# Nine of the 22 gate/value pairs of a feed-forward up-projection by seven block products in place of eight

## The chip, the cores and the metric

The kernel runs on one core of one Trainium2 chip. The metric is device time in microseconds (us) of one execution. Three runs of the kernel before took 861.26, 861.86 and 863.12 us; the median is 861.86 us.

## The reference

One block of a network on x of 512 rows (SEQ) and 1024 columns (D). A mixer (an mLSTM, an S5 state-space branch and their output product) takes up the first half of the time and is not touched. After it comes a feed-forward part with 2816 hidden channels, which are 22 groups of 128; the convolution has three taps along the rows:

```python
h = _standardize(x) * (1.0 + sc2) + sh2
val, gate = jnp.split(h @ w_ffn_up, 2, axis=-1)
gate = jax.nn.gelu(_causal_dwconv(gate, w_ffn_conv, b_ffn_conv))
f = (gate * val) @ w_ffn_down
x = _layer_norm(ALPHA * x + (1.0 + g2) * f, ln2_gain, ln2_bias)
```

All data are 32-bit floats.

## The kernel before, in words

**Products in three parts.** TensorE multiplies operands in the type fp32r. To keep the precision of 32 bits, each operand is split into a high part and a rest: ScalarE casts it (L221, `split_into`), VectorE subtracts the cast from the original (L210, `sub`). `mm3` (L241 to L244) then makes high x high, high x rest and rest x high, all added into one PSUM bank. A weight tile is loaded from DRAM into a `w` tile (SyncE starts the load, L192) and split into `wh` and `wl` (`wsplit`), 128 partitions x 1024 each.

**The up-projection.** `h2` holds the eight transposed activation tiles (128 channels x 512 rows each, as high part and rest; in the pools `s5b`, `s5h` and `hx`). A *unit* is one group of 128 output channels: `up_mm` makes 8 contraction blocks x 3 matmuls of 512 columns. Two units make a *pair* j: first the gate unit 2j+1 into a bank `acc`, then the value unit 2j into a bank `hd`. The first four units (pairs 0 and 1, `early`) are made in two halves of 256 columns, since the second half of the rows is transposed later.

`gate_half` (L1180 on) takes the gate from PSUM: ScalarE copies it to SBUF (L1184) and makes the last tap with its bias (L1186), VectorE adds two taps (L202), then `gelu2` (L561 to L565) goes ScalarE Square (L562), VectorE, ScalarE Tanh (L564), VectorE. `val_half` multiplies by the value bank (L207) and splits the product into a high part and a rest, which stay in SBUF until the down-projection reads them.

```python
for j in range(NF):
    ...
    for u in (2 * j + 1, 2 * j):
        ...
            w = wsplit(h["wup"][u])
            ou[u] = bank("acc" if u % 2 else "hd")
            up_mm(ou[u], w, slice(0, 512))
        if u % 2:
            gg = gate_half(j, ou[u])
    val_half(j, gg, ou[2 * j])
    if 8 <= j < 16:
        ada2_step(1)
```

`ada2_step` makes an eighth of a modulation vector on VectorE (two L202 passes into `s5h`); `grow` (at `G2J`) turns that vector into a row for all partitions, which scales the down-projection's weights.

**The down-projection.** `tail_product` goes through the 22 blocks in order and multiplies the scaled weights with the stored products, into all eight PSUM banks; the last eight blocks' weights are held resident, and the result goes through the norm row tile by row tile.

**What sets the order.** The program order of each engine is settled when the kernel is built, by the framework's scheduler from the order of the code, and each engine then works strictly in that order, with semaphore waits between engines. Pools limit how far engines run ahead: `w` 2 buffers, `wh` and `wl` 3 each, `gab` 4, `hh` 7, and of the eight PSUM banks `acc` 2, `s5` 2, `hd` 4.

## Time and profile before

| | |
|---|---|
| median of 3 runs | 861.86 us (861.26 to 863.12) |
| the profiled execution: its span | 862.0 us |
| TensorE (PE) busy | 828.5 us, 96% |
| VectorE (DVE) busy | 607.1 us, 70% |
| ScalarE (ACT) busy | 368.6 us, 43% |
| GpSimd (POOL) busy | 98.0 us, 11% |
| DMA queue, share of 16 engines | 36.0% |
| chain that ended last | PE 76%, DVE 11%, ACT 4%, DMA 4% |

The span goes from the first to the last instruction of one execution under the profiler; what lies around it is within the spread of the three runs, so the span is compared with the median as it stands. Busy shares are means over stages with different limits. The chain is the work that ended last, followed back from the last instruction to what released each step. In a timeline a row gives start, length, engine, line, operation, output <- inputs, and in brackets the idle time of the engine before it and what ended that.

### The profile page before, as it was taken

The numbers are of one execution on the slowest core, as the hardware profiler recorded it, in microseconds if no ns is written. First come the engines' busy times: TensorE is split into PE (matmuls) and PEld (weight loads), VectorE is DVE, ScalarE is ACT, GpSimd is POOL, SyncE is SP. The second block draws the span as 40 slices with busy tenths as digits, with TensorE's granted clock in tenths as the row PEclk, the third lists the DMA queues.
The fourth block names the chain that finished last, engine by engine and source line by source line (L and its number), as shares of the span: only waits on it lengthen the run. The fifth ranks groups of instructions, "written<-read, shape, count | busy, mean of one in ns | idle before, by whom it ended". The sixth has DMA issues, their size and how long they took to land.

```text
span 862.0 us, 11353 instructions
## 1 busy us (share of the span) xinstructions
PE 828.5 (96%) x4106; PEld 669.2 (78%) x4106; DVE 607.1 (70%) x1144; ACT 368.6 (43%) x589; POOL 98.0 (11%) x255
## 2 busy tenths in 40 slices
PE   3999999999999999999999999999999999999996
PEld 1777868778777778888887988888888878888785
DVE  5557978788689774578978767556777675878144
ACT  4454573564556442232334555444444444333000
POOL 2781211122022100000002200000000000000000
PEclk9999999999999999999999999999999999999998
DMA  9832132122222233568655023224444232445011
GB/s 336 288 132 86 53 101 62 45 85 62 79 60 87 86 123 122 196 203 294 210 191 177 2 74 102 94 98 147 146 147 137 86 120 74 171 163 169 11 49 49
DMA packets 45415, 105.94 MB, mean 123 GB/s; under 512 B 13360, under 2 KB 14256, under 8 KB 45360
## 3 DMA queue, kind: packets, MB, share of 16 engines
q1 hardware_dynamic: 45360, 105.23, 36.0%
q8 instruction: 32, 0.52, 0.2%
q14 instruction: 23, 0.19, 0.1%
HBM read 101.01 MB, written 2.10 MB: 120 GB/s over the span
## 4 chain that ended last, share of the span: by engine, by line
PE 76%; DVE 11%; ACT 4%; DMA 4%; issue 2%; SPq 2%; POOL 0%; DVEq 0%; ACTq 0%; POOLq 0%
PE acc L242 11%; PE acc L243 11%; PE acc L244 11%; PE hd L242 11%; PE hd L243 11%; PE hd L244 11%; DVE hh L202 2%; SPq L192 2%; DVE s5h L207 1%; PE s L242 1%; PE s L244 1%; PE s L243 1%; DVE wl L210 1%; PE s L612 1%; DMA w<-in_wmix 1%
## 5 line engine op out<-in xcount | busy, mean ns | idle before, releaser
L221 ACT CAST wh<-w 128x1024 fp32r<-128x1024 f32 (+2 forms) x103 | 103.2, 1003 | 144.0 <-PE acc L243 111.5
L210 DVE TENSOR_TENSOR wl<-w,wh 128x1024 fp32r<-128x1024 f32 (+2 forms) x103 | 120.5, 1172 | 60.8 <-ACT wh L221 60.1
L242 PE MATMUL acc<-hp,wh 128*128 128x512 f32 x256 | 103.4, 405 | 0.5 <-ACT hx L785 0.5
L244 PE MATMUL acc<-hp,wl 128*128 128x512 f32 x256 | 102.1, 399 | 0.0
L243 PE MATMUL acc<-hp,wh 128*128 128x512 f32 x256 | 102.1, 399 | 0.0
L242 PE MATMUL hd<-s5b,wh 128*128 128x512 f32 (+1 forms) x168 | 63.4, 380 | 0.7 <-ACT s5b L1169 0.5
L243 PE MATMUL hd<-s5b,wh 128*128 128x512 f32 (+1 forms) x168 | 63.6, 379 | 0.2 <-DVE s5b L210 0.2
L244 PE MATMUL hd<-s5b,wl 128*128 128x512 f32 (+1 forms) x168 | 63.3, 378 | 0.0
L242 PEld LDWEIGHTS acc<-hp,wh 128*128 128x128 f32 x256 | 48.2, 189 | 14.7 <-issue 3.7
L202 DVE SCALAR_TENSOR_TENSOR hh<-hh,hh 128x512 f32<-128x512 f32 x52 | 35.9, 691 | 31.2 <-ACT hh L564 14.7
L244 PEld LDWEIGHTS acc<-hp,wl 128*128 128x128 f32 x256 | 48.4, 189 | 11.2 <-issue 0.4
L243 PEld LDWEIGHTS acc<-hp,wh 128*128 128x128 f32 x256 | 48.4, 189 | 10.8 <-issue 0.4
L202 DVE SCALAR_TENSOR_TENSOR s5h<-hh,k,s5h 128x512 f32<-128x512 f32 x56 | 39.3, 746 | 4.7 <-DMA hh<-in_wa 4.6
L242 PEld LDWEIGHTS hd<-s5b,wh 128*128 128x128 f32 x168 | 31.3, 188 | 7.6 <-ACT s5b L1169 0.8
L243 PEld LDWEIGHTS hd<-s5b,wh 128*128 128x128 f32 x168 | 31.7, 189 | 7.0 <-DVE s5b L210 0.6
L244 PEld LDWEIGHTS hd<-s5b,wl 128*128 128x128 f32 x168 | 31.6, 188 | 6.4
L202 DVE SCALAR_TENSOR_TENSOR hh<-hh,k,hh 128x512 f32<-128x512 f32 x44 | 33.0, 751 | 4.5 <-ACT hh L1186 3.6
L1024 POOL TENSOR_SCALAR mov<-mov 128x1 f32<-128x1 f32 x6 | 3.7, 624 | 276.2 <-ACT s L1023 159.6
L244 PE MATMUL acc<-hx,wl 128*128 128x512 f32 x84 | 33.1, 394 | 0.0
L242 PE MATMUL acc<-hx,wh 128*128 128x512 f32 x84 | 33.1, 394 | 0.0
L243 PE MATMUL acc<-hx,wh 128*128 128x512 f32 x84 | 33.1, 394 | 0.0
L244 PE MATMUL acc<-s5b,wl 128*128 128x512 f32 x80 | 31.6, 395 | 0.5 <-DVE wl L210 0.5
(547 smaller groups left out, 2053.1 us busy)
## 6 DMA issues: line engine op xcount, KB each, us to landing
w<-in_wup SPq DMA_DIRECT2D x44, 512.0 KB, 3.2
hh<-in_wa SPq DMA_DIRECT2D x64, 256.0 KB, 4.2
w<-in_win SPq DMA_DIRECT2D x30, 512.0 KB, 3.2
w<-in_wfd SPq DMA_DIRECT2D x22, 512.0 KB, 3.3
hb<-in_wa SPq DMA_DIRECT2D x16, 512.0 KB, 7.4
w<-in_wglu SPq DMA_DIRECT2D x8, 512.0 KB, 3.3
w<-in_wdn SPq DMA_DIRECT2D x8, 512.0 KB, 3.3
w<-in_wmix SPq DMA_DIRECT2D x8, 512.0 KB, 4.2
```

The costliest lines, as they stand in the source:

```text
L192: return nc.sync.dma_start(o, i)
L202: V.scalar_tensor_tensor(o, i0, s, i1, op0=op0, op1=op1)
L207: V.tensor_tensor(o, a, b, op=op)
L210: V.tensor_tensor(o, a, b, op=ALU.subtract)
L221: A.copy(hi, x)
L242: T.matmul(o, lhsT=wh, rhs=xh, start=first, stop=False)
L243: T.matmul(o, lhsT=wh, rhs=xl, start=False, stop=False)
L244: T.matmul(o, lhsT=wl, rhs=xh, start=False, stop=last)
L612: T.matmul(o, lhsT=F[:, ri, pr, :], rhs=XB[:, ri, pr].rearrange("p g k -> p (g k)"), start=ri == 0, stop=False)
L1024: GP.tensor_scalar(v[:, 2:3], v[:, 0:1], v[:, 1:2], EPS * D, op0=ALU.add, op1=ALU.add)
```

## The change

The two units of a pair have the same eight activation tiles as their other operand. With the contraction cut into two halves and the 512 rows cut into two halves, a pair is a product of two 2 x 2 block matrices: the weights A11, A12 (gate, first and second half of the contraction), A21, A22 (value) and the activations B. For nine pairs (`FAST`) `fast_pair` makes it by seven block products, in Winograd's form of Strassen's scheme, in place of eight; a product (`prod`) is 4 contraction blocks x 3 matmuls of 256 columns.

- Four combinations of the weights per pair (S1 to S4), each 128x512, on GpSimd (`gtt`); the weights are loaded into the pool `gab`. Seven weight blocks are then split (`half`), each 128x512, in the pools `wh` and `wl` in turn.
- Four combinations of the activations, made and split once when pair 2 begins (`x_combos`), from raw activations that are now kept (`xraw`); they fill four buffers of `hp` (their splits are `xd`).
- Order of the products: a = A11 B11; copy of a into bank b by ScalarE; c = S3 X3; copy of c to SBUF; b += S2 X2; then VectorE adds b and c into bank d; a += A12 B21; b += S1 X1; VectorE adds b and c again (v); d += A22 X4; b += S4 B22. The gate is a (first half of the rows) and b (second half), the value d and v. Bank b is an `acc` bank, d an `s5` bank, by the parity of j; a and c are `hd` banks.
- `gate_half` reads the gate from PSUM where it stands in one bank, and copies it from two banks where it doesn't; its first tap is shortened at the edge in place of two zeros ahead; the buffer of the GELU is now an `hd` bank.
- The products of pairs 0 to 7 go to DRAM (`spill`) in place of SBUF, since `hp` is taken, and come back in the down-projection (`act_at`), which now takes the blocks 8 to 17 first, then 0 to 7, then 18 to 21, and splits the returned ones there.
- The `ada2_step` calls move from pairs 8 to 15 to pairs 6, 9, 12, 15, 18 (two) and 19 (two), and `grow` from pair 19 to 20.

```diff
-G2J = 19
+G2J = 20
+FAST = (5, 7, 8, 10, 11, 13, 14, 16, 17)
+MODS = (6, 9, 12, 15, 18, 18, 19, 19)
+NSP = 8
...
+            if hv:
+                if j % 2 == 0:
+                    xraw.append(big((P, 2, 512), F32, "gab"))
+                a = xraw[j // 2][:, j % 2, sl]
+            else:
+                a = hh(256)
...
+    spill = dp.tile([NSP * P, 512], F32, name="spill")
+    gtile = [bank("acc"), bank("acc")]
+    vtile = [bank("s5"), bank("s5")]
+
     def gate_half(j, og):
-        gb_ = hh(514)
-        GP.memset(gb_[:, 0:2], 0.0)
-        A.copy(gb_[:, 2:514], og)
         a = hh()
-        A.activation(a, og, AF.Identity, bias=col("fb", j), scale=col("fw", 44 + j))
+        if len(og) == 1:
+            g = og[0]
+        else:
+            g = hh()
+            for i in range(2):
+                A.copy(g[:, 256 * i:256 * i + 256], og[i][:, 0:256])
+        A.activation(a, g, AF.Identity, bias=col("fb", j), scale=col("fw", 44 + j))
         for q in range(2):
-            stt(a, gb_[:, q:q + 512], col("fw", 22 * q + j), a)
+            d = 2 - q
+            stt(a[:, d:], g[:, :512 - d], col("fw", 22 * q + j), a[:, d:])
         gg = hh()
-        gelu2(gg, a, hh)
+        gelu2(gg, a, lambda: bank("hd"))
...
     def val_half(j, gg, ov):
-        tt(gg, ov, gg)
-        gp_.append(pair_of(gg, "hp" if j < 8 else "hb" if j < 13 else "s5b" if j < 15 else "hx" if j < 18 else "gab"))
+        if len(ov) == 1:
+            tt(gg, ov[0], gg)
+        else:
+            for i in range(2):
+                sl = slice(256 * i, 256 * i + 256)
+                tt(gg[:, sl], ov[i][:, 0:256], gg[:, sl])
+        if j < NSP:
+            dma(spill[j * P:(j + 1) * P, :], gg)
+            gp_.append(None)
...
+    def half(src):
+        o = big((P, 2, 512), F32R, next(optag))
+        A.copy(o[:, 0], src)
+        sub(o[:, 1], src, f32(o[:, 0]))
+        return o
+
+    optag = iter(("wh", "wl") * (4 * NF))
+    xd = []
+
+    def x_combos():
+        for _ in range(4):
+            xd.append([big((P, 2, 2, 256), F32R, "hp") for _ in range(2)])
+        lo_ = slice(0, 256)
+        hi_ = slice(256, 512)
+        xk = [xraw[k // 2][:, k % 2, :] for k in range(KD)]
+        for k in range(KD):
+            gtt(xk[k][:, lo_], f32(h2[k][0])[:, lo_], f32(h2[k][1])[:, lo_], ALU.add)
+        for k in range(4):
+            gtt(xk[k][:, lo_], xk[k][:, hi_], xk[k][:, lo_], ALU.subtract)
+            gtt(xk[k][:, hi_], xk[k + 4][:, hi_], xk[k][:, hi_], ALU.subtract)
+        for k in range(4):
+            tt(xk[k + 4][:, hi_], xk[k + 4][:, hi_], xk[k][:, lo_], ALU.subtract)
+            tt(xk[k + 4][:, lo_], xk[k + 4][:, lo_], xk[k + 4][:, hi_], ALU.subtract)
+        for i, (kh, th) in ((2, (0, hi_)), (1, (1, hi_)), (0, (0, lo_)), (3, (1, lo_))):
+            for n, x in enumerate(xd[i]):
+                r = xraw[2 * kh + n][:, :, th]
+                A.copy(x[:, 0], r)
+                sub(x[:, 1], r, f32(x[:, 0]))
+
+    def xq(kh, th):
+        return [[y[:, 256 * th:256 * th + 256] for y in h2[4 * kh + k]] for k in range(4)]
+
+    def xc(i):
+        return [[xd[i - 1][k // 2][:, e, k % 2, :] for e in range(2)] for k in range(4)]
+
+    def prod(o, w, x, first=False):
+        for k in range(4):
+            sl = slice(k * P, (k + 1) * P)
+            for i, (p, y) in enumerate(((0, 0), (0, 1), (1, 0))):
+                T.matmul(o[:, 0:256], lhsT=w[:, p, sl], rhs=x[k][y], start=first and k + i == 0, stop=k == 3 and i == 2,
+                         skip_group_check=True)
+
+    def fast_pair(j):
+        wg_, wv_ = (wload(h["wup"][u], tag="gab") for u in (2 * j + 1, 2 * j))
+        a11, a12, a21, a22 = wg_[:, :512], wg_[:, 512:], wv_[:, :512], wv_[:, 512:]
+        b, d = gtile[j % 2], vtile[j % 2]
+        a, c = bank("hd"), bank("hd")
+        w1 = half(a11)
+        gtt(a21, a11, a21, ALU.subtract)
+        s3 = half(a21)
+        w4 = half(a22)
+        gtt(a22, a22, a21, ALU.subtract)
+        s2 = half(a22)
+        w2 = half(a12)
+        gtt(a11, a22, a11, ALU.add)
+        s1 = half(a11)
+        gtt(a12, a12, a22, ALU.subtract)
+        s4 = half(a12)
+        prod(a, w1, xq(0, 0), True)
+        A.copy(b[:, 0:256], a[:, 0:256])
+        prod(c, s3, xc(3), True)
+        cs = hh(256)
+        A.copy(cs, c[:, 0:256])
+        prod(b, s2, xc(2))
+        tt(d[:, 0:256], b[:, 0:256], cs, ALU.add)
+        prod(a, w2, xq(1, 0))
+        prod(b, s1, xc(1))
+        v = hh(256)
+        tt(v, b[:, 0:256], cs, ALU.add)
+        prod(d, w4, xc(4))
+        prod(b, s4, xq(1, 1))
+        gg = gate_half(j, (a, b))
+        val_half(j, gg, (d, v))
...
+        if j == NS // 2:
+            x_combos()
+        if j in FAST:
+            fast_pair(j)
+        else:
+            ou = {}
+            for u in (2 * j + 1, 2 * j):
+                if u in pre:
+                    ou[u] = pre[u]
+                else:
+                    w = wsplit(h["wup"][u])
+                    ou[u] = (gtile if u % 2 else vtile)[j % 2]
+                    up_mm(ou[u], w, slice(0, 512))
+                if u % 2:
+                    gg = gate_half(j, (ou[u],))
+            val_half(j, gg, (ou[2 * j],))
+        ada2_step(MODS.count(j))
...
+    down = list(range(NSP, 18)) + list(range(NSP)) + list(range(18, NF))
+    got = {}
+
+    def act_at(k):
+        for kk in range(k, min(k + 3, NF)):
+            j = down[kk]
+            if kk in got:
+                continue
+            if j >= NSP:
+                got[kk] = gp_[j]
+                continue
+            x = hh()
+            dma(x, spill[j * P:(j + 1) * P, :])
+            got[kk] = pair_of(x, "s5h" if j < 4 else "hx" if j < 7 else "hb")
+        return got[k]
+
+    tail_product(act_at, [h["wfd"][j] for j in down], g2, "hh", NF, 8, [("s5b", "s5b")] * 2 + [("hp", "hp")] * 4 + [("hb", "hb")] * 2, finish2, FDB, first)
```

How the instructions move, at three places. Each row is line, operation, output <- inputs and the output's shape; line numbers of the changed kernel are some 4 to 120 higher.

ScalarE, where one pair ends and the next begins, before: `wh_1239` is the cast of the next pair's gate weights, `wh_1247` that of its value weights, `acc_1226` the gate bank of the pair that ends.

```order
L221 CAST wh_1239_6020<-w_1238_6018 128x1024
L221 CAST hb_1220_5924<-hh_1214_5886 128x512
L221 CAST wh_1247_6064<-w_1246_6062 128x1024
L1184 COPY hh_1227_5964<-acc_1226_5939 128x512
L1186 ACTIVATE hh_1228_5967<-acc_1226_5939,k_1_61 128x512
L562 ACTIVATE hh_1230_5972<-hh_1228_5967 128x512
L564 ACTIVATE hh_1230_5972<-hh_1230_5972 128x512
L221 CAST wh_1254_6105<-w_1253_6103 128x1024
```

In the change, the same place between the fast pairs 10 and 11: `gab_1224` and `gab_1225` are the weights of pair 11, `hd_1208` and `acc_1056` banks a and b of pair 10, `hd_1226`, `hd_1227` and `acc_1057` banks a, c and b of pair 11.

```order
L1226 CAST wl_1229_6181<-gab_1225_6173 128x512
L1226 CAST wh_1232_6191<-gab_1224_6171 128x512
L1202 COPY hh_1220_6154<-hd_1208_6036 128x256
L1226 CAST wl_1231_6188<-gab_1225_6173 128x512
L1202 COPY hh_1220_6154<-acc_1056_4895 128x256
L1226 CAST wl_1233_6195<-gab_1224_6171 128x512
L1203 ACTIVATE hh_1219_6153<-hh_1220_6154,k_1_63 128x512
L566 ACTIVATE hd_1222_6161<-hh_1219_6153 128x512
L568 ACTIVATE hd_1222_6161<-hd_1222_6161 128x512
L1226 CAST wh_1234_6199<-gab_1224_6171 128x512
L1283 COPY acc_1057_4896<-hd_1226_6175 128x256
L1286 COPY hh_1235_6227<-hd_1227_6176 128x256
```

The last but one row, the copy of pair 11's first product into its bank b, stands behind the whole gate of pair 10, up to its Tanh (L568).

TensorE at the start of pair 11 in the change, with the waits: a is `hd_1226`, c is `hd_1227`, b is `acc_1057`. The wait on ScalarE ahead of the first row into `acc_1057` is for that copy.

```order
L1263 MATMUL hd_1226_6175<-s5b_1011_4724,wh_1228_6177 128x256 x3
L1263 MATMUL hd_1227_6176<-hp_1098_5199,wl_1229_6181 128x256 [waits Activation_49]
L1263 MATMUL hd_1227_6176<-hp_1098_5199,wl_1229_6181 128x256 x5
L1263 MATMUL hd_1227_6176<-hp_1099_5200,wl_1229_6181 128x256 x6
L1263 MATMUL acc_1057_4896<-hp_1096_5197,wl_1231_6188 128x256 [waits Activation_49]
L1263 MATMUL acc_1057_4896<-hp_1096_5197,wl_1231_6188 128x256
L1263 MATMUL acc_1057_4896<-hp_1096_5197,wl_1231_6188 128x256 [waits DVE_49]
L1263 MATMUL acc_1057_4896<-hp_1096_5197,wl_1231_6188 128x256 x3
L1263 MATMUL acc_1057_4896<-hp_1097_5198,wl_1231_6188 128x256 x6
L1263 MATMUL hd_1226_6175<-s5h_1012_4725,wh_1232_6191 128x256
```

There is no other product between the second one (into c) and the third (into b).

VectorE ahead of the sum into d of pair 10 (the last row), in the change; `acc_1057` and `hd_1199` belong to the gate of normal pair 9, `gab_1206` and `gab_1207` are the weights of pair 10, `s5h_1155` and `s5h_1156` the modulation vector.

```order
L206 SCALAR_TENSOR_TENSOR hh_1197_5982<-acc_1057_4896,k_1_63,hh_1197_5982 128x511
L214 TENSOR_TENSOR wh_1213_6049<-gab_1207_6034,wh_1213_6049 128x512
L206 SCALAR_TENSOR_TENSOR hd_1199_5987<-hd_1199_5987,hh_1197_5982 128x512
L214 TENSOR_TENSOR wh_1215_6056<-gab_1206_6032,wh_1215_6056 128x512
L206 SCALAR_TENSOR_TENSOR hh_1198_5986<-hd_1199_5987,hh_1197_5982 128x512
L214 TENSOR_TENSOR wl_1214_6052<-gab_1206_6032,wl_1214_6052 128x512
L211 TENSOR_TENSOR hh_1198_5986<-s5_1059_4898,hh_1198_5986 128x512
L206 SCALAR_TENSOR_TENSOR s5h_1155_5668<-hh_1204_6026,k_15_92,s5h_1155_5668 128x512
L214 TENSOR_TENSOR hb_1203_6023<-hh_1198_5986,hb_1203_6023 128x512
L206 SCALAR_TENSOR_TENSOR s5h_1156_5669<-hh_1205_6029,k_15_92,s5h_1156_5669 128x512
L214 TENSOR_TENSOR wl_1216_6060<-gab_1206_6032,wl_1216_6060 128x512
L211 TENSOR_TENSOR s5_1058_4897<-acc_1056_4895,hh_1217_6088 128x256
```

Before, the same stretch of VectorE between two units' splits:

```order
L210 TENSOR_TENSOR wl_1240_6021<-w_1238_6018,wh_1239_6020 128x1024
L210 TENSOR_TENSOR hb_1220_5924<-hh_1214_5886,hb_1220_5924 128x512
L202 SCALAR_TENSOR_TENSOR s5h_1189_5755<-hh_1221_5927,k_15_90,s5h_1189_5755 128x512
L202 SCALAR_TENSOR_TENSOR s5h_1190_5756<-hh_1222_5930,k_15_90,s5h_1190_5756 128x512
L210 TENSOR_TENSOR wl_1248_6065<-w_1246_6062,wh_1247_6064 128x1024
L202 SCALAR_TENSOR_TENSOR hh_1228_5967<-hh_1227_5964,k_1_61,hh_1228_5967 128x512 x2
L202 SCALAR_TENSOR_TENSOR hh_1230_5972<-hh_1230_5972,hh_1228_5967 128x512
L202 SCALAR_TENSOR_TENSOR hh_1229_5971<-hh_1230_5972,hh_1228_5967 128x512
L207 TENSOR_TENSOR hh_1229_5971<-hd_1234_5983,hh_1229_5971 128x512
```

In the change the sum stands behind the gate steps of pair 9 and five of pair 10's weight splits; the split of a unit's weights in one piece of 1024 columns has become pieces of 512.

## Rows read from the trace of the kernel before

**Rows 1.** Of the page: busy time of each engine, and the chain by engine.

```profile
PE 828.5 (96%) x4106; PEld 669.2 (78%) x4106; DVE 607.1 (70%) x1144; ACT 368.6 (43%) x589; POOL 98.0 (11%) x255
...
PE 76%; DVE 11%; ACT 4%; DMA 4%; issue 2%; SPq 2%; POOL 0%; DVEq 0%; ACTq 0%; POOLq 0%
```

**Rows 2.** 506 to 696 us: length, busy PE PEld DVE ACT POOL, PEclk, DMA share, GB/s.

```profile
506.00:696.00 190.00, 189.48 (x818) 153.15 (x817) 128.45 (x162) 90.61 (x128) 1.70 (x17) 1.00 0.36 122
```

**Rows 3.** Timeline of TensorE: first matmuls of two successive value units.

```profile
546.13 0.39 PE L242 MATMUL hd<-s5b,wh 128*128 128x512 f32 x1
...
557.27 0.39 PE L242 MATMUL hd<-s5b,wh 128*128 128x512 f32 x1
```

**Rows 4.** The same, of the units made in halves of 256 columns.

```profile
480.69 0.28 PE L242 MATMUL hd<-s5b,wh 128*128 128x256 f32 x1
...
486.37 0.28 PE L242 MATMUL hd<-s5h,wh 128*128 128x256 f32 x1
```

**Rows 5.** Groups of ScalarE, 0 to 470 us: busy us, mean ns, idle before.

```profile
L221 ACT CAST hp<-hx 128x512 fp32r<-128x512 f32 x16 | 9.9, 621 | 8.9 <-DVE hx L207 8.7
...
L806 ACT ACTIVATE hh<-hx,k 128x512 f32<-128x512 f32 x8 | 6.5, 809 | 0.0
...
L316 ACT COPY hh<-s 128x256 f32<-128x256 f32 x8 | 3.0, 374 | 6.9 <-PE s L313 6.9
```

**Rows 6.** Timeline of ScalarE and VectorE: one gate, 547 to 553 us.

```profile
547.58 0.78 ACT L1186 ACTIVATE hh<-acc,k 128x512 f32<-128x512 f32 x1
...
548.47 1.54 DVE L202 SCALAR_TENSOR_TENSOR hh<-hh,k,hh 128x512 f32<-128x512 f32 x2
...
550.79 0.69 DVE L202 SCALAR_TENSOR_TENSOR hh<-hh,hh 128x512 f32<-128x512 f32 x1 [0.78 <-ACT hh L562]
...
551.52 0.63 ACT L564 ACTIVATE hh<-hh 128x512 f32<-128x512 f32 x1 [0.76 <-DVE hh L202]
...
552.18 0.69 DVE L202 SCALAR_TENSOR_TENSOR hh<-hh,hh 128x512 f32<-128x512 f32 x1 [0.70 <-ACT hh L564]
```

**Rows 7.** The same of VectorE, whole span.

```profile
L210 DVE TENSOR_TENSOR wl<-w,wh 128x1024 fp32r<-128x1024 f32 x40 | 48.8, 1220 | 43.5 <-ACT wh L221 43.5
L202 DVE SCALAR_TENSOR_TENSOR hh<-hh,k,hh 128x512 f32<-128x512 f32 x44 | 33.0, 751 | 4.5 <-ACT hh L1186 3.6
L202 DVE SCALAR_TENSOR_TENSOR hh<-hh,hh 128x512 f32<-128x512 f32 x44 | 30.4, 692 | 29.2 <-ACT hh L564 14.7 <-ACT hh L562 14.6
...
L210 DVE TENSOR_TENSOR hp<-hh,hp 128x512 fp32r<-128x512 f32 x16 | 11.0, 687 | 4.1 <-ACT hp L221 4.1
...
L210 DVE TENSOR_TENSOR s5b<-hh,s5b 128x256 fp32r<-128x256 f32 x5 | 1.9, 420 | 0.1
```

**Rows 8.** The same of GpSimd, whole span.

```profile
L345 POOL TENSOR_TENSOR k<-k,hh 128x128 f32<-128x128 f32 x2 | 0.9, 461 | 0.1
...
L345 POOL TENSOR_TENSOR k<-k,hh 128x64 f32<-128x64 f32 x2 | 0.7, 358 | 0.0
```

**Rows 9.** Timeline of GpSimd and VectorE, at 97 and at 145 us.

```profile
97.00 3.11 POOL L786 TENSOR_SCALAR hx<-hx,k 128x512 f32<-128x512 f32 x1 [12.68 <-ACT hx L785]
...
145.12 0.69 POOL L786 TENSOR_SCALAR hx<-hx,k 128x512 f32<-128x512 f32 x1 [4.05 <-ACT hx L785]
...
145.26 1.62 DVE L210 TENSOR_TENSOR wl<-w,wh 128x1024 fp32r<-128x1024 f32 x1
```

**Rows 10.** Timeline of VectorE and TensorE, 506 to 508 us.

```profile
506.22 1.23 DVE L210 TENSOR_TENSOR wl<-w,wh 128x1024 fp32r<-128x1024 f32 x1 [6.91 <-ACT wh L221]
...
507.50 0.50 PE L244 MATMUL acc<-s5b,wl 128*128 128x512 f32 x1 [0.52 <-DVE wl L210]
```

**Rows 11.** Timeline of TensorE at 161 us.

```profile
161.61 0.46 PE L612 MATMUL s<-k,s5b 128*128 128x128 f32 x2 [1.65 <-DVE k L210]
```

**Rows 12.** Windows view around the wait of rows 11, columns as in rows 2.

```profile
152.00:172.00 20.00, 18.35 (x94) 15.66 (x93) 14.84 (x23) 9.33 (x17) 3.46 (x5) 0.91 0.18 48
```

**Rows 13.** Timeline of VectorE in the down-projection.

```profile
809.00 1.29 DVE L210 TENSOR_TENSOR s5b<-hh,s5b 128x512 fp32r<-128x512 f32 x2 [11.41 <-PE hd L244]
```

More of the change, by code (lines that the diff above doesn't have):

```diff
@@ L162, in _build @@
     ps = ctx.enter_context(tc.tile_pool(name="ps", bufs=1, space=PSUM))
+    dp = ctx.enter_context(tc.tile_pool(name="dp", bufs=1, space=bass.MemoryType.DRAM))
     uid = [0]
@@ L939, in row_w, with grow @@
         return [r[:, :512], r[:, 512:]]
-    def grow(i, factor):
+    def grow(i, factor, tag="s5"):
         g = row(i)
         for n in range(2):
-            o = bank("s5")
+            o = bank(tag)
             for e, x in enumerate(pair_of(acc2[2 + i][n], "hh")):
@@ L1092, in one @@
             tk = slice(t * P, (t + 1) * P)
-            mm3(bk[t][n][:, c_], acts[k][0][:, tk], acts[k][1][:, tk], wh[:, sl], wl[:, sl], k == 0, k == nk - 1 and c_.stop == 512)
+            x = acts(k) if callable(acts) else acts[k]
+            mm3(bk[t][n][:, c_], x[0][:, tk], x[1][:, tk], wh[:, sl], wl[:, sl], k == 0, k == nk - 1 and c_.stop == 512)
         last = []
@@ L1151, in finish1 @@
         yield
-    h2 = []
+    h2, xraw = [], []
     def h2tr(hv):
@@ L1163, in h2tr @@
                 T.transpose(pt[:, t * P:(t + 1) * P], x[:, (j % 4) * P:(j % 4 + 1) * P], ident)
-            a = hh(256)
+            if hv:
[4 more added lines that the diff above has]
+                a = hh(256)
             if j % 2:
@@ new lines, in val_half @@
+        if j < NSP:
+            dma(spill[j * P:(j + 1) * P, :], gg)
+            gp_.append(None)
+        else:
+            gp_.append(pair_of(gg, "hb" if j < 14 else "s5b" if j < 15 else "hx" if j < 18 else "gab"))
+    def half(src):
[24 more added lines that the diff above has]
+                sub(x[:, 1], r, f32(x[:, 0]))
@@ L1211, in _build @@
         if j == G2J:
-            g2 = grow(1, 0.5)
+            g2 = grow(1, 0.5, "hd")
         if j >= FJ:
-            first.append(scaled(h["wfd"][len(first)], g2, None))
-        ou = {}
-        for u in (2 * j + 1, 2 * j):
-            if u in pre:
-                ou[u] = pre[u]
-            else:
-                w = wsplit(h["wup"][u])
-                ou[u] = bank("acc" if u % 2 else "hd")
-                up_mm(ou[u], w, slice(0, 512))
-            if u % 2:
-                gg = gate_half(j, ou[u])
-        val_half(j, gg, ou[2 * j])
-        if 8 <= j < 16:
-            ada2_step(1)
+            first.append(scaled(h["wfd"][NSP + len(first)], g2, None))
+        if j == NS // 2:
[7 more added lines that the diff above has]
+                    ou[u] = pre[u]
+                else:
+                    w = wsplit(h["wup"][u])
[5 more added lines that the diff above has]
+        ada2_step(MODS.count(j))
     l2 = []
@@ L1238, in finish2 @@
         yield
-    tail_product(gp_, h["wfd"], g2, "hh", NF, 8, [("s5b", "s5b")] * 2 + [("hp", "hp")] * 4 + [("hb", "hb")] * 2, finish2, FDB, first)
+    down = list(range(NSP, 18)) + list(range(NSP)) + list(range(18, NF))
[13 more added lines that the diff above has]
+    tail_product(act_at, [h["wfd"][j] for j in down], g2, "hh", NF, 8, [("s5b", "s5b")] * 2 + [("hp", "hp")] * 4 + [("hb", "hb")] * 2, finish2, FDB, first)
 def kernel(**inputs):
```

## The prediction

> **What bounds the kernel now.** First the page's busy times and its chain of waits: TensorE is busy for 96% of the span and holds 76% of the chain [rows 1]. Then the stretch of the up-projection, 506 to 696 us, alone: TensorE 189.48 of 190 us at the full clock, VectorE only 128.45, ScalarE 90.61, GpSimd 1.7 [rows 2]. So time is saved there by fewer matmul columns alone, and lost wherever TensorE has to wait. The price of a matmul is taken from start to start, since the listed 0.4 us overlap: 48 matmuls of 512 columns lie between the two rows of [rows 3], 11.14 us, which is one pair; 48 of 256 columns take 5.68 us in [rows 4], 0.1183 us each. This is little more than half, so the narrow matmuls hide their weight loads.
>
> **A. What is removed.** A pair by seven products has 84 matmuls of 256 columns, 84 x 0.1183 = 9.94 us for 11.14. Nine pairs: 9 x 1.20 = **-10.8 us**, if TensorE never waits. One product takes 12 x 0.1183 = 1.42 us.
>
> **B. Two fast pairs in succession (7-8, 10-11, 13-14, 16-17: four turns).** In a fast pair the third product adds to bank b, which must first receive a copy of the first product. ScalarE's order puts that copy of pair 11 behind the whole gate of pair 10, and TensorE's order has nothing else to do. Counted from the last product of pair 10, this chain is: copy of 256 columns 0.37, a weight cast 0.62, the biased activation 0.81 [rows 5]; from the first convolution step to the end of Tanh 3.68 (548.47 to 551.52 + 0.63) [rows 6]; one more cast 0.62 and the copy 0.37; four handovers of 0.1, as 548.36 to 548.47 [rows 6]. Sum 6.9 us. TensorE has two products, 2.84, to run meanwhile: it waits 4.1 us, more than the 2.4 that two fast pairs save. A GpSimd add can hold up VectorE inside the chain, for 0 to 1.1 us (below); I take half: 4.6 x 4 = **+18.4** (16.4 to 20.8).
>
> **C. Normal pair, then fast (9-10, 12-13, 15-16).** Bank b may take its second addend, in the fifth product, only when VectorE has read it (the sum into d). VectorE is strictly in order, and before that sum stand the gates of the two pairs before. From the end of pair 8: its gate's first VectorE step can start at 0.37 + 0.62 + 0.81 + handovers = 2.1 us. Then, with [rows 7]: four convolution steps 3.00, four GELU steps 2.77, two value products 1.53 (one of 512 columns, two of 256), five weight splits 3.44, two activation splits 1.37, two accumulations 1.50, the sum 0.42: 14.0 us. Two waits for ScalarE inside the first gate, 0.78 and 0.70 [rows 6], are not covered. Total 17.6; TensorE is ready at 11.14 + 4 x 1.42 = 16.8. Wait 0.8 us, before GpSimd is counted.
>
> GpSimd makes four 128x512 combinations per fast pair. The trace has no such instruction; adds of 64 and 128 columns take 0.358 and 0.461 us [rows 8], 1.6 ns per column, which continues to 1.08 us for 512 (an estimate; a one-input pass of this size takes 0.69 at least, 3.11 at most [rows 9]). GpSimd itself has time, 4.3 of 9.9 us. But the engines disturb each other: at 145.26 VectorE took 1.62 us for a split that takes 1.22, in the shadow of a GpSimd pass, and at 97.00 GpSimd took 3.11 us beside a full VectorE [rows 9]. Three combinations fall into the 17.6 us and may cost 0 to 3.3; half gives 2.4 us of wait, three times 7.2. At 6-7 VectorE has no activation splits (both values are spilled), only 0.5 is left; at 4-5 nothing. **+7.7** (2.4 to 14.5).
>
> The Trainium skill, SBUF — State Buffer, section "Who interferes with whom", has a rule: a VectorE instruction with two inputs in SBUF contends with a GpSimd instruction that reads SBUF, and the loser blocks fully. By it every weight split meets every combination head on, and the upper ends would hold: +35.3 for B and C in place of +26.1. The two rows at 145 and 97 us agree with it; how often they meet the row cannot say.
>
> **D. The combinations of the activations**, made once as pair 2 begins: VectorE 8 x 0.42 + 8 x 0.69 = 8.9 us [rows 7], behind GpSimd's 16 half-size adds. Before the change VectorE idles 6.91 us at this place, and TensorE then waits 0.52 [rows 10]. 8.9 does not go into 6.9: **+2.0** (0 to 3.5, if GpSimd ends late).
>
> **E. The clock.** After TensorE had waited 1.65 us at 160 [rows 11] the granted clock averaged 0.91 over 20 us [rows 12]: 20 x 0.09 = 1.8 us of work lost at 1.2 in place of 2.4 GHz. After 0.52 us of waiting [rows 10] it stayed at 1.00 [rows 2]. The waits of B are longer than either: 4 x 1.8 = **+7.2** (0, or 14.4 if those of C do it too).
>
> **What costs nothing.** The eight spills move 2 MB each way through queues that are a third busy [rows 2]. Their eight splits move into the down-projection, 8 x 0.69 = 5.5 us; the cover is VectorE's idle time of 11.41 us before 809 [rows 13]; without it these are +5.5. The moved ada steps put 3.0 us into pairs 18 and 19 each, where VectorE uses some 7.5 of 11.1. The copy that normal pairs lose was off the path.
>
> **Sum.** -10.8 + 18.4 + 7.7 + 2.0 + 7.2 = +24.5 us. The profiled execution spans 862.0, the median of the runs is 861.86: **886.5 us**. All lower ends: -10.8 + 16.4 + 2.4 = +8, 870. All upper ends: +42.4, 904.
>
> **Rivals.**
> 1. *TensorE stays the bound, faster:* -10.8 + 2.0, 853 us. ScalarE's 43% and the idle VectorE speak for it; the place of the copy behind Tanh speaks against. Point of decision: the chain of B must fall below 2.84 + 2.40 = 5.2 us; the rows give 6.9. Chance 0.11.
> 2. *Waits without company:* no disturbance by GpSimd and no fall of the clock; 870 us. For it: a starved GpSimd pass left VectorE alone at 97 us [rows 9]. Against: [rows 12]. Chance 0.22.
> 3. *GpSimd and VectorE shut each other out each time:* B and C at their upper ends, -10.8 + 20.8 + 14.5 + 2.0 + 7.2 = +33.7, 896 us. This is what the rule of the SBUF page would make here. For it: 1.62 for 1.22. Against: part of VectorE's steps read PSUM. Chance 0.15.
> 4. *The change does less than it says,* or a wait that I have not seen (a spill that holds a load, the tail): near 862 or past 904. Chance 0.07.
>
> My forecast has 0.45. The range 867 to 902 holds it, rival 2 and most of rival 3. Faster by over 0.2% (1.7 us, about what a measurement of this kernel can tell from no change): 0.12; within 0.2%: 0.03; slower: 0.85.
>
> **What would show it.** Right: matmuls of 256 columns at 0.118 us; at four places TensorE waits 4 to 5 us before a product into b, released by ScalarE's copy; shorter waits for VectorE's sum before fifth products; TensorE's clock at half after the long ones; ScalarE and VectorE each far from full. Wrong: third products that start within 1 us of the second, or a fast pair of 10 us after another. Then B has failed and the time is near 853.

## The result and the profile after

The changed kernel takes 898.97 us (median of 4 runs, 896.23 to 899.49), the kernel before beside it 862.49 us (861.26 to 863.82): a ratio of 1.0417, 95% interval 1.0397 to 1.0437. The change costs 36.5 us. The profiled execution spans 897.3 us, where the one before spans 862.0. Its page gives, in place of [rows 1]:

```profile
PE 831.3 (93%) x4430; PEld 685.5 (76%) x4430; DVE 661.8 (74%) x1232; ACT 389.7 (43%) x656; POOL 161.4 (18%) x285
...
PE 59%; DVE 21%; ACT 6%; DMA 4%; issue 4%; POOL 3%; SPq 2%; DVEq 0%; ACTq 0%; POOLq 0%
```

TensorE is busy for about as long as before (831.3 us, some of it at half clock), and its part of the chain has fallen by 17 points, most of which VectorE has (11% to 21%). Where the 35 us between the two spans came from is read from TensorE's timeline, at the first matmul of a pair (the times are us from the start of the execution, or the length of a stretch):

| | before | after | difference |
|---|---|---|---|
| first matmul of pair 2 | 506.24 | 509.74 | +3.5 |
| pairs 2 to 4 | 34.33 | 37.92 | +3.6 |
| pairs 5 to 17 (nine of them fast) | 144.73 | 171.47 | +26.7 |
| from pair 18 to the end | 176.7 | 178.2 | +1.5 |

Of the first row 2.7 us are a wait that is read below; the other 0.8 had come up before that wait, in the untouched first part, which differs by more than that from one execution to the next. In pairs 5 to 17 the list of TensorE's waits has two rows (total us, times, longest):

```profile
PE acc L1263 <- ACT acc L1283: 20.3, 5, 5.3
PE acc L1263 <- DVE s L211: 5.9, 5, 1.6
```

The first is the copy of the first product into bank b: 5.04, 5.29, 5.30 and 4.15 us at the four turns from a fast pair to the next, 19.8 us, and 0.53 once more. The second is VectorE's sum into d: 1.55, 1.56 and 1.60 us at pairs 10, 13 and 16, 0.96 at pair 7, 0.27 at pair 5. Here is the turn from pair 10 to 11, from the timeline of all engines (start, length, engine, line; several instructions in a row are one line with their count):

```profile
619.72 4.99 POOL L349 TENSOR_TENSOR gab<-gab,gab 128x512 f32<-128x512 f32 x3
...
620.32 3.26 DVE L214 TENSOR_TENSOR wl<-gab,wl 128x512 fp32r<-128x512 f32 x2
...
621.89 0.81 ACT L1203 ACTIVATE hh<-hh,k 128x512 f32<-128x512 f32 x1
...
623.51 2.53 DVE L206 SCALAR_TENSOR_TENSOR hh<-hh,k,hh 128x510 f32<-128x510 f32 x2
626.13 0.60 ACT L566 ACTIVATE hd<-hh 128x512 f32<-128x512 f32 x1 [3.43 <-DVE hh L206]
...
627.50 0.58 ACT L568 ACTIVATE hd<-hd 128x512 f32<-128x512 f32 x1 [0.77 <-DVE hd L206]
...
628.50 0.38 ACT L1283 COPY acc<-hd 128x256 f32<-128x256 f32 x1
...
628.93 1.44 PE L1263 MATMUL acc<-hp,wl 128*128 128x256 f32 x5 [5.29 <-ACT acc L1283]
```

This is the chain of part B: biased activation, two convolution steps, Square, Tanh, and only then the copy (L1283) for which TensorE has waited 5.29 us. The rows also show GpSimd's company: three adds, which take 1.29 us each at best (one at 618.34), take 4.99, and the two weight splits beside them 3.26 us in place of 1.37, the first convolution steps 2.53 in place of 1.50. After the wait the clock is low (windows: start:end, length, busy time of PE, PEld, DVE, ACT, POOL, granted clock, DMA share, GB/s):

```profile
500.00:520.00 20.00, 15.44 (x84) 13.15 (x83) 17.21 (x29) 10.45 (x17) 4.11 (x5) 0.83 0.46 165
...
610.00:626.00 16.00, 12.09 (x101) 11.56 (x99) 15.41 (x19) 7.78 (x15) 7.58 (x5) 1.00 0.31 99
626.00:634.00 8.00, 5.07 (x26) 5.07 (x27) 3.72 (x8) 2.90 (x6) 1.22 (x1) 0.57 0.19 66
634.00:650.00 16.00, 16.00 (x90) 13.77 (x90) 11.00 (x16) 8.93 (x15) 3.04 (x3) 1.00 0.30 99
```

```profile
545.00:720.00 175.00, 148.65 (x965) 136.53 (x964) 127.86 (x176) 84.64 (x154) 48.24 (x33) 0.93 0.27 88
```

The mean of 0.57 over 8 us means 3.4 us lost at one turn; 0.93 over the 175 us of all the fast pairs means some 12 us, where [rows 2] had 1.00. So pairs 5 to 17 close to about 1 us: -10.8 for the columns, +26.2 for the waits, +12 for the clock is +27.4, measured +26.7. That it closes so well is in part luck: some of the low clock lies inside the waits and is counted twice, and on the other side each wait costs some 0.16 us more than its row says, since the row of a matmul lasts 0.28 us where one starts every 0.118.

The loss at pair 2 is that of part D. On ScalarE the casts of the activations' combinations (L1250) stand ahead of pair 2's weight cast (L225), and wait for GpSimd's adds; on VectorE their splits stand ahead of the weight split:

```profile
501.38 0.62 ACT L1250 CAST hp<-gab 128x512 fp32r<-128x512 f32 x1 [2.96 <-POOL gab L349]
...
503.75 0.62 ACT L1250 CAST hp<-gab 128x512 fp32r<-128x512 f32 x1 [1.44 <-POOL gab L349]
...
506.88 4.29 DVE L214 TENSOR_TENSOR hp<-gab,hp 128x512 fp32r<-128x512 f32 x7
508.65 1.04 ACT L225 CAST wh<-w 128x1024 fp32r<-128x1024 f32 x1
...
509.74 0.50 PE L246 MATMUL acc<-s5b,wh 128*128 128x512 f32 x1 [2.69 <-ACT wh L225]
...
511.09 1.21 DVE L214 TENSOR_TENSOR wl<-w,wh 128x1024 fp32r<-128x1024 f32 x1
...
512.35 0.79 PE L248 MATMUL acc<-s5b,wl 128*128 128x512 f32 x1 [1.87 <-DVE wl L214]
```

Waits of 2.69 and 1.87 us in place of the 0.52 of [rows 10], and the 0.83 of the window 500 to 520 above is another 3.4 us.

### The profile page after: what moved, and what is told of

Read it like the earlier page. It is cut to its first block, busy times and chain, and to the rows that moved or that the text cites. A ratio compares the mean times of both kernels' runs of the same rounds, so it can differ in the third digit from the quotient of the medians.

```text
span 897.3 us, 12212 instructions
## 1 busy us (share of the span) xinstructions
PE 831.3 (93%) x4430; PEld 685.5 (76%) x4430; DVE 661.8 (74%) x1232; ACT 389.7 (43%) x656; POOL 161.4 (18%) x285
## 4 chain that ended last, share of the span: by engine, by line
PE 59%; DVE 21%; ACT 6%; DMA 4%; issue 4%; POOL 3%; SPq 2%; DVEq 0%; ACTq 0%; POOLq 0%
PE acc L246 8%; PE acc L248 8%; PE acc L247 8%; PE hd L246 6%; PE hd L247 6%; PE hd L248 6%; DVE hh L206 5%; DVE wl L214 3%; PE acc L1263 3%; POOL gab L349 3%; PE s L246 2%; PE s L248 2%; PE s L247 2%; SPq L196 2%; DVE wh L214 1%
## 5 line engine op out<-in xcount | busy, mean ns | idle before, releaser
L225 ACT CAST wh<-w 128x1024 fp32r<-128x1024 f32 (+2 forms) x85 | 84.5, 997 | 122.9 <-PE acc L247 73.2
L214 DVE TENSOR_TENSOR wl<-w,wh 128x1024 fp32r<-128x1024 f32 (+2 forms) x85 | 100.3, 1183 | 39.2 <-ACT wh L225 38.3
L248 PEld LDWEIGHTS acc<-hp,wl 128*128 128x128 f32 x256 | 48.2, 188 | 11.3 <-issue 0.4
L247 PEld LDWEIGHTS acc<-hp,wh 128*128 128x128 f32 x256 | 48.4, 189 | 10.8 <-issue 0.4
L349 POOL TENSOR_TENSOR gab<-gab,gab 128x512 f32<-128x512 f32 (+1 forms) x31 | 42.4, 1378 | 64.6 <-DMA gab<-in_wup 30.6
L1263 PE MATMUL acc<-hp,wl 128*128 128x256 f32 x120 | 21.5, 343 | 20.0 <-ACT acc L1283 19.8
L206 DVE SCALAR_TENSOR_TENSOR hh<-hd,hh 128x512 f32<-128x512 f32 (+3 forms) x40 | 24.4, 609 | 18.2 <-ACT hd L568 9.1
L1263 PEld LDWEIGHTS acc<-hp,wl 128*128 128x128 f32 x120 | 19.7, 248 | 21.0 <-ACT acc L1283 20.6
L214 DVE TENSOR_TENSOR wh<-gab,wh 128x512 fp32r<-128x512 f32 x32 | 26.5, 830 | 10.5 <-ACT wh L1226 10.5
L247 PE MATMUL hd<-s5b,wh 128*128 128x512 f32 (+1 forms) x88 | 32.2, 367 | 0.5 <-DVE s5b L214 0.5
L246 PE MATMUL hd<-s5b,wh 128*128 128x512 f32 (+1 forms) x88 | 31.8, 367 | 0.7 <-ACT s5b L1179 0.5
L225 ACT CAST hb<-hh 128x512 fp32r<-128x512 f32 (+3 forms) x44 | 24.7, 561 | 17.7 <-DVE hh L206 11.0
L248 PE MATMUL hd<-s5b,wl 128*128 128x512 f32 (+1 forms) x88 | 31.9, 364 | 0.0
L214 DVE TENSOR_TENSOR wl<-gab,wl 128x512 fp32r<-128x512 f32 x31 | 28.5, 920 | 2.3 <-ACT wl L1226 1.5
```

The costliest lines, as they stand in the source:

```text
L206: V.scalar_tensor_tensor(o, i0, s, i1, op0=op0, op1=op1)
L214: V.tensor_tensor(o, a, b, op=ALU.subtract)
L225: A.copy(hi, x)
L246: T.matmul(o, lhsT=wh, rhs=xh, start=first, stop=False)
L247: T.matmul(o, lhsT=wh, rhs=xl, start=False, stop=False)
L248: T.matmul(o, lhsT=wl, rhs=xh, start=False, stop=last)
```

## The experiments

The theory after the first reading was that the order of the queues makes the waits, and the waits make the clock fall. Times are medians; the kernel before, run beside each group, took 861.0 to 861.8 us. Where a span is used, it is that of the profiled execution. The untouched first 485 us differ by up to 3 us from one execution to the next, so stretches are compared from pair to pair.

**1. The copy ahead of the gate.**

```diff
         A.activation(a, g, AF.Identity, bias=col("fb", j), scale=col("fw", 44 + j))
+        yield
...
-        A.copy(b[:, 0:256], a[:, 0:256])
+        cb = A.copy(b[:, 0:256], a[:, 0:256])
...
         tt(d[:, 0:256], b[:, 0:256], cs, ALU.add)
+        if late:
+            with tc.issue_after(cb.ins):
+                run_late()
```

`run_late` makes the rest of the gate of the pair before; `issue_after` queues its ScalarE instructions behind the copy.

> The copy of bank b of the second fast pair is put ahead of the Square and Tanh of the pair before on ScalarE (the rest of that gate is emitted after the sum into d); products, columns and splits are the same. Theory (the order on ScalarE makes the wait, and the wait makes the clock fall): the four turn waits of 4.15 to 5.30 us (19.8 in all) fall to under 1 us each, the clock's half-speed stretches inside the fast pairs (23.9 us, 11.3 lost) go, and VectorE, with some 29.9 us of work for 31 us of products in three pairs, gives back a few us as longer waits for the sum: 866 to 873 us. Rival 1 (GpSimd's adds make the chain long, not the order): the waits stay over 3 us, 887 us or more. Rival 2 (the clock falls for what TensorE does in fast pairs, not for the waits): waits go, half-speed stretches stay, 877 to 882 us.

Measured: 881.54 us, ratio 1.0226 (1.0203 to 1.025): 20.1 us above the kernel before beside it, where the change was 36.5 above. The turn waits are 0, 2.47, 2.47 and 0.80 us, and pairs 5 to 17 take 152.6 us in place of 171.5, with 1.7 us lost to the clock. So the order was most of it, and rival 1 falls. Rival 2's figure is met but not its mechanism: the clock did not stay low. The 8 us beyond the theory's range are waits that are left: 2.5 us for sums at pairs 5, 7 and 8, 1.9 for copies from normal to fast, a wait of 1.84 us behind pair 20 (as in run 12), and the two of 2.47, the first of which reads:

```profile
613.31 4.99 POOL L349 TENSOR_TENSOR gab<-gab,gab 128x512 f32<-128x512 f32 x3
...
613.92 3.26 DVE L214 TENSOR_TENSOR wl<-gab,wl 128x512 fp32r<-128x512 f32 x2
...
618.34 0.62 ACT L1241 CAST wh<-gab 128x512 fp32r<-128x512 f32 x1 [2.03 <-POOL gab L349]
618.86 0.37 ACT L1298 COPY acc<-hd 128x256 f32<-128x256 f32 x1
...
619.28 1.68 PE L1278 MATMUL acc<-hp,wl 128*128 128x256 f32 x12 [2.47 <-ACT acc L1298]
```

The copy (L1298) now stands behind the cast of the seventh weight block, and that cast has waited 2.03 us for GpSimd.

**2. TensorE kept busy in the wait.**

```diff
         A.copy(cs, c[:, 0:256])
+        if j - 1 in FAST:
+            for _ in range(3):
+                prod(d, w1, xq(0, 0), True)
```

> Order as in the change, but at the four turns TensorE makes 36 more matmuls of 256 columns (4.26 us) while it would wait; their result in bank d is overwritten by the sum that comes after. Theory (the clock falls because TensorE waits): the waits before b shrink to about 1 us, the half-speed stretches inside the fast pairs go, and since the filling takes the time of the waits the gain is the clock's 11.3 us: 884 to 889 us. Rival 2 (the clock falls for what the fast pairs do): no gain or a loss, 896 to 900 us, with the half-speed stretches still there.

Measured: 889.43 us, ratio 1.0322 (1.0303 to 1.0341), 28.0 us above the kernel before beside it in place of 36.5, and 0.4 us above the theory's range. At the same turn as above the window now reads:

```profile
626.00:634.00 8.00, 6.76 (x56) 6.35 (x56) 5.00 (x9) 3.70 (x8) 0.09 (x1) 1.00 0.21 70
664.00:676.00 12.00, 10.76 (x82) 10.00 (x81) 7.51 (x12) 7.15 (x13) 1.30 (x1) 1.00 0.27 90
```

The granted clock is 1.00 through all the fast pairs, though the same products run and the gate is as late as before: the fillings (4.26 us at each of four turns) and the waits that are left (8.9 us) together are about as long as the waits of the change. Pairs 5 to 17 take 163.4 us, 8.0 less than in the change. So some 8 us of the loss are the clock's, and the clock falls because TensorE waits.

**3. The preparations alone.**

```diff
-FAST = (5, 7, 8, 10, 11, 13, 14, 16, 17)
+FAST = ()
```

> No pair by seven products; all the rest of the change stays: the combinations of the activations, made and split though nobody reads them, the spills, the moved modulation steps, the gate read from PSUM. Theory (the combinations delay pair 2's weight splits by some 4 us and the clock falls after that, 7.1 us in all, and the rest of the change costs 1.5): 869 to 872 us. Rival (that loss belongs to the fast pairs, and the preparations lie beside other work): 861 to 864 us.

Measured: 869.77 us, ratio 1.0089 (1.0074 to 1.0104), with the waits of 2.70 and 1.88 us at pair 2 and no other between there and pair 18. From pair 2 to pair 4 it takes 3.9 us more than before, from pair 5 to pair 17 as long as before, and from pair 18 on 0.7 more. So the loss at pair 2 comes from the preparations, whether or not a fast pair follows.

**4 and 5. Where the combinations of the activations stand.** In the first of two runs they are only emitted later in the code, in the second they are queued behind pair 2's splits:

```diff
-        if j == NS // 2:
+        if j == 4:
             x_combos()
```

```diff
-        if j == NS // 2:
-            x_combos()
+        if j == NS // 2 + 1:
+            with tc.issue_after(mark["A"].ins), tc.issue_after(mark["V"].ins):
+                x_combos()
```

> The combinations of the activations are emitted as pair 4 begins, not as pair 2 begins, all else as in the change. Theory (at pair 2 they stand ahead of its weight splits on ScalarE and VectorE; in pairs 2 to 4 both engines have idle time for them): pair 2 starts without the two waits of 2.69 and 1.87 us and without the half-speed stretch at 522 us; 889 to 892 us. Rival (VectorE's work is only moved, and is waited for elsewhere, or the later loads of pair 5's weights make it late): 895 to 899 us.

> The combinations of the activations are now really queued behind the weight splits of pair 2 on ScalarE and VectorE (the run that only emitted them later left both queues' order as it was). Theory (at pair 2 they stand ahead of its weight splits, and their GpSimd adds are waited for): the waits of 2.69 and 1.87 us and the half-speed stretch at 520 us go, and pairs 2 to 4 have room for the 9 us of VectorE: 890 to 894 us. Rival (the work is only moved): the waits come back in pairs 3 to 5 and the time stays at 896 to 900 us.

Measured: 897.34 us (ratio 1.0418, 1.0396 to 1.0439) and 901.45 us (1.0467, 1.0452 to 1.0483). The first says nothing on the theory: the scheduler, which orders by what it holds to be ready, left both queues as they were, and the waits at pair 2 are 2.69 and 1.42 us. The second did move the work, and the theory falls: TensorE's timeline has no wait but the 0.53 of before at pair 2, and at pair 3:

```profile
526.48 0.79 PE L250 MATMUL acc<-s5b,wl 128*128 128x512 f32 x1 [6.52 <-DVE wl L228]
```

VectorE has the gates of pairs 0 and 1 to make up for in pairs 2 and 3 (it is busy for all of the 7 us from 520 on, with steps of these gates and splits of the combinations), so 9 us more are as much in the way there. Only in three parts behind the splits of pairs 2, 3 and 4 (runs 9 to 12 below) was there no wait for them: there pairs 2 to 4 take 34.3 us, as before.

**6. The weight combinations on VectorE.**

```diff
-        gtt(a21, a11, a21, ALU.subtract)
+        tt(a21, a11, a21, ALU.subtract)
```

and so for the other three.

> The four weight combinations of a fast pair are made by VectorE, not by GpSimd; all else as in the change. It measures what GpSimd's company costs. In the change VectorE's 63 weight splits of fast pairs take 55.0 us, 11.8 more than 63 undisturbed ones; the nine pairs' combinations are 24.8 us of work for VectorE. Theory (the order sets the turn waits; the disturbance is a second, smaller term): splits back at 0.69 us, turn waits of 3 to 4 us in place of 5.3 because two splits and two convolution steps there lose their 2.9 us of disturbance, but longer waits for the sum, 2.5 to 3.5 us in place of 1.6: 891 to 902 us. Rival (GpSimd's company is the main cause): turn waits under 2 us, under 888 us.

Measured: 893.9 us, ratio 1.039 (1.0371 to 1.0409). With GpSimd idle the splits take their undisturbed time (groups of VectorE, xcount, busy and mean ns), first in the change, then here:

```profile
L214 DVE TENSOR_TENSOR wl<-gab,wl 128x512 fp32r<-128x512 f32 x30 | 27.8, 928 | 2.3 <-ACT wl L1226 1.5
L214 DVE TENSOR_TENSOR wh<-gab,wh 128x512 fp32r<-128x512 f32 x31 | 25.8, 834 | 10.5 <-ACT wh L1226 10.5
```

```profile
L214 DVE TENSOR_TENSOR wh<-gab,wh 128x512 fp32r<-128x512 f32 x31 | 21.2, 684 | 4.2 <-ACT wh L1226 4.2
L214 DVE TENSOR_TENSOR wl<-gab,wl 128x512 fp32r<-128x512 f32 x30 | 20.5, 685 | 3.3 <-ACT wl L1226 3.3
```

The turn waits fall from 5.3 to 3.33 us each and the waits for the sum rise from 1.6 to 2.26, as the theory has it. So the order alone, without disturbance, makes some 3.3 us of a turn, and GpSimd's company the other two. That the time falls by so little has a second reason, which the theory did not have: the granted clock over the fast pairs is lower than in the change (0.91 for 0.93), since here the waits of 2.26 us for the sum, too, are each followed by a stretch at half clock:

```profile
545.00:720.00 175.00, 154.18 (x977) 142.67 (x976) 131.73 (x212) 86.39 (x156) 0.00 (x0) 0.91 0.27 92
```

**7. No turn.**

```diff
-FAST = (5, 7, 8, 10, 11, 13, 14, 16, 17)
-MODS = (6, 9, 12, 15, 18, 18, 19, 19)
+FAST = (5, 7, 9, 11, 13, 15, 17)
+MODS = (6, 8, 10, 12, 14, 16, 18, 19)
```

> Seven fast pairs, each followed by a normal one (5, 7, 9, 11, 13, 15, 17), the modulation steps in the normal pairs; all else as in the change. Theory (the loss sits at the turns from fast to fast): no turn waits, no half-speed stretch after 530 us; 861.9 - 7 x 1.2 + 7.1 (combinations of the activations) + 1.5 (tail) + seven waits of 0.3 to 1.6 us for the copy or the sum: 864 to 872 us. Rival (every fast pair costs about as much, 26.7 us for nine in the change): 861.9 + 8.6 + 7 x 3.0, 888 to 894 us.

Measured: 872.66 us, ratio 1.0138 (1.0122 to 1.0153), 0.7 us above the theory's range and far from the rival. There is no turn wait and no low clock after pair 2, but pairs 5 to 17 take 146.8 us, 2.1 more than before, where the columns alone would take 136.3: waits of 0.2 to 1.5 us for the copy, the sum or a split at each fast pair eat what it saves. The turns were not all.

**8. Three queues at once.**

```diff
-        s4 = half(a12)
...
-        A.copy(cs, c[:, 0:256])
+        cc = A.copy(cs, c[:, 0:256])
+        with tc.issue_after(cc.ins):
+            s4 = half(a12)
```

together with the edits of runs 1 and 5.

> Three changes of queue order and none of work: the copy of bank b ahead of the gate (as in the first run), the combinations of the activations behind pair 2's splits, and the cast of the seventh weight block behind the two copies on ScalarE, since in the first run that cast waited for GpSimd with the copy behind it (2.47 us, twice). Theory (orders of queues, not the amount of work, make the loss): 881.5 - 6 for the activations - 6 for those waits and the clock: 866 to 871 us. Rival (VectorE, with 118.7 busy us of 140 in the first run, is now the bound): 875 us or more, with more waits for the sum.

Measured: 881.66 us, ratio 1.024 (1.0211 to 1.027). Of the turn waits one of 1.57 us is left, but pair 3 waits 6.29 us as in run 5, and the copies from normal to fast wait up to 1.43 us. The rival's figure is met; whether VectorE's amount of work or its order is behind it, this run does not say.

**9 and 10. The first products early.** `fast_pair` is cut in two (`fast_a`: loads, the first two products and both copies), eight pairs are fast, and the combinations of the activations come in three parts:

```diff
-FAST = (5, 7, 8, 10, 11, 13, 14, 16, 17)
+FAST = (7, 8, 10, 11, 13, 14, 16, 17)
+COMB = (3, 4, 5)
...
+        if j + 1 in FAST:
+            nxt[j + 1] = fast_a(j + 1)
         prod(d, w4, xc(4))
         prod(b, s4, xq(1, 1))
```

The second of the two also queues the value unit of a normal pair behind them:

```diff
+                    if u % 2 == 0 and j + 1 in FAST:
+                        with tc.issue_after(mark["T"].ins):
+                            up_mm(ou[u], w, slice(0, 512))
```

> Eight fast pairs (7, 8, 10, 11, 13, 14, 16, 17). The first two products of the second pair of a turn are issued before the last two of the first pair, so copies and gate have two products more of cover; the combinations of the activations are cut into three parts, queued behind the splits of pairs 2, 3 and 4. Theory (all the loss is order; TensorE has work to run while ScalarE and VectorE catch up): no turn waits over 1 us, no stretch at half clock after 480 us, pair 3 no more than 2 us late: 861.9 - 9.6 + some 6 us of small waits for copies and sums at normal to fast + 1.5 (tail) + 2: 858 to 866 us. Rival (VectorE is the bound, since three pairs have some 30 us of work for it, disturbance included, in 31): the waits move to the sums and splits, and it is 868 us or more.

> As the run before, and the value unit of a normal pair is queued behind the first two products of the fast pair that follows, so that the copies into bank b have 5.6 us more of cover there too. Theory (order): the waits for the copy and the sum at normal to fast (0.4 to 1.6 us each in the runs so far) go, 2 to 6 us less than the run before: 854 to 862 us. Rival (VectorE is the bound): the two weight blocks that are now wanted earlier come late in their turn, and the time is within 1.5 us of the run before or above it.

Measured: 878.61 us (ratio 1.0197, 1.0179 to 1.0215) and 886.09 us (1.0281, 1.0262 to 1.03). Both times the rival's range. The turns are covered, and the waits have moved to sums and splits; in the second run TensorE's longest waits in sum are:

```profile
PE acc L1270 <- DVE s L212: 9.5, 4, 2.9
PE acc L1270 <- ACT acc L1282: 4.1, 3, 1.8
```

and ScalarE's own, from 545 to 700 us:

```profile
ACT hd L569 <- DVE hh L207: 14.3, 9, 2.2
ACT wl L1229 <- POOL gab L352: 14.0, 8, 3.1
```

So after two repairs of the order the chain goes through GpSimd: casts wait for its combinations, VectorE's splits for the casts.

**11. The same without GpSimd's part.** Run 9 without the four weight combinations: the raw blocks are split and multiplied in their place, so that part of the computation is left out.

```diff
-        gtt(a22, a22, a21, ALU.subtract)
         s2 = half(a22)
         w2 = half(a12)
-        gtt(a11, a22, a11, ALU.add)
         s1 = half(a11)
-        gtt(a12, a12, a22, ALU.subtract)
         s4 = half(a12)
```

> The run with eight fast pairs and the first products early, without GpSimd's four weight combinations per fast pair: the raw weight blocks are split and multiplied in their place, so that part of the computation is left out. ScalarE's casts, VectorE's splits and TensorE's products stay the same in number. Theory (what is left of the loss is GpSimd: its passes stand in a chain with the splits, and disturb VectorE): 878.6 falls to 856 to 866 us, splits at 0.69 us. Rival (VectorE's own amount of work is the bound): 870 us or more, with the waits for the sums still there.

Measured: 860.06 us, ratio 0.9994 (0.998 to 1.0007), 18.6 us less than run 9. In the windows of the two kernels, run 9 first:

```profile
545.00:690.00 145.00, 130.76 (x843) 117.28 (x842) 107.11 (x154) 73.31 (x135) 43.38 (x31) 0.98 0.27 92
```

```profile
545.00:690.00 145.00, 143.62 (x948) 130.14 (x947) 111.75 (x177) 84.66 (x151) 0.00 (x0) 1.00 0.31 104
```

The same casts, splits and products are made, VectorE does more per microsecond (111.75 busy us of 145, where run 9 has 107.11), and TensorE is busy for 143.62 of 145 us at the full clock. So VectorE's own amount of work is not the bound. From the start of pair 5 to the value unit of pair 18 this run takes 142.5 us, run 9 161.3, the kernel before 150.3: with GpSimd out of the chain eight fast pairs save 7.8 of the 9.6 us that the columns promise. The median is that of the kernel before all the same, in part because the stretch from there to the end takes 174.9 us in place of 171.1. How much of the 18.6 us is disturbance and how much the chain of casts behind the combinations, the run cannot say, since both go together.

**12. Four fast pairs far apart.** The change's own `fast_pair`, `FAST = (8, 11, 14, 17)`, the combinations of the activations in three parts as in run 9.

> Four fast pairs only, each with two normal pairs ahead of it (8, 11, 14, 17), in the change's own form, and the combinations of the activations in three parts behind the splits of pairs 2, 3 and 4, where the run with the early products showed no wait for them. Theory (seven products pay where VectorE and ScalarE have caught up; two normal pairs leave VectorE over 6 us of room): no turn, waits of under 0.5 us per fast pair, no half clock after 480 us: 861.9 - 4.8 + 2 + 0 to 1.5 (tail) = 858 to 861 us, faster than before by a little. Rival (a fast pair costs more than it saves wherever it stands): 864 us or more.

Measured: 866.45 us, ratio 1.0062 (1.0049 to 1.0075), outside the theory's range and in the rival's. TensorE's two largest waits in sum from pair 5 on:

```profile
PE acc L1270 <- DVE s L212: 2.8, 4, 1.2
PE acc L249 <- DVE hh L207: 1.8, 1, 1.8
```

The four pairs take 10.2, 11.2, 10.1 and 11.2 us, where a normal one takes 11.14: two save 1 us, two wait 1.2 us for the sum and save nothing. Beyond that, from pair 18 to the end it takes 181.6 us, 4.9 more than before. There the down-projection waits 1.84 us for VectorE, and a stretch at half clock follows. The prediction had put the moved modulation steps (pairs 18 and 19, `grow` at 20) at nothing; they cost little in run 3 (+0.7) and in the change (+1.5), and the same wait, of 1.8 to 2.5 us, stands in runs 1, 8, 9, 10 and 11. That the steps are the cause was not tried by itself.

No version that computes the whole came out under the kernel before.

## Why the prediction was right, and where it was off

The time lies in the range (867 to 902), on the side that was forecast; the forecast was +24.5 us, the measured difference is +36.5. By its own terms:

- **A, the columns (-10.8): right.** Matmuls of 256 columns start 0.118 us apart, and run 11 shows the saving where nothing waits.
- **B, the turns (+18.4): right, 19.8 measured**, at the four places and for the copy that the prediction named; run 1 shows the order as their cause. Inside the term the shares were off: undisturbed a turn waits some 3.3 us (run 6) where 4.1 was worked out, and GpSimd adds 2 where 0.55 was taken. That the total agrees is partly luck, since the two misses cancel.
- **C, normal to fast (+7.7): right, 6.5 measured.** The three waits were 1.6 us each in place of 2.4, that at pair 7 0.96 (and 0.53 for the copy) in place of 0.5.
- **D, the combinations of the activations (+2.0): mis-sized, 6.3 measured** (2.7 of waiting and 3.6 in pairs 2 to 4). "8.9 does not go into 6.9" counted VectorE's time alone. Two things were missing: on ScalarE their casts stand ahead of pair 2's weight cast and wait for GpSimd, and the waits of 2.69 and 1.87 us bring the clock down, which part E charged to the turns only.
- **E, the clock (+7.2): the mechanism right (run 2), the size off.** The window at 626 loses 3.4 us, where 1.8 was taken from the window of [rows 12], which followed a wait of 1.65 us; it is some 12 us in the fast pairs, of which run 2 gives back 8; the 3.4 at pair 2 stand in D's figure.
- **"What costs nothing":** the tail costs 1.5 us in the change, and 3.5 to 6 in runs 1 and 9 to 12, where the down-projection's first product waits for VectorE.

Sum with the measured terms: -10.8 + 19.8 + 6.5 + 6.3 + 12 + 1.5 = +35.3, and 0.8 of the untouched part, against +35.3 between the spans. Of the 12 us by which the forecast was too low, E makes 4.8, D 4.3 and the tail 1.5; B and C together make 0.2.

Of the rivals, the first (TensorE stays the bound) needed the chain of B under 5.2 us; it took 2.84 + 5.3 = 8.1. The second (no disturbance, no fall of the clock) is excluded by the rows at 620 and at 626 us. The third gives 896 us, nearest to the time, for a reason that the rows bear out in half: it had B and C at their upper ends by full exclusion, +35.3, and they are +26.3. The rule that it drew on, from the Trainium skill, SBUF — State Buffer, section "Who interferes with whom", is that the two engines' shared ports are an exclusive lock and the loser blocks fully. The trace agrees nearly where the engines meet, except that both sides lose and not one: at 620 us VectorE loses 1.9 us on two splits and 1.0 on a convolution step, GpSimd 1.1 on three adds, together 4.0 of the 4.4 us (620.32 to 624.71) in which both run. Rival 3 supposed that they meet each time, and they do not: over the nine pairs the splits take 53.6 us in the groups above where 61 undisturbed ones would take 41.8, which is 0.35 us for each of the 34 combinations in that view. The convolution steps of 510 columns (nine, 1.08 us in the mean where run 6 has 0.75) and the modulation steps (six, 1.07 for 0.75) lose 4.9 us more, so that a combination costs VectorE some 0.5 us, a third of its own length.

## What to carry to other kernels

Fewer columns on the bound engine pay only if the work that prepares them stays off its path; before such a change, follow the longest chain from one product's result to the next product's operand, in the order of each queue, and set it against the work that TensorE has in between. An instruction that merely copies can be the most expensive one if it stands behind a chain of other engines. A wait of a few microseconds can cost more than its length, since the clock may fall after it; and a place in the code is no place in a queue, so that an experiment on order has to be checked in the queue before its time is read.
